# Strassen's seven products for q and z of five heads in a hybrid attention block

## The chip, the cores and the metric

The kernel runs on one core of a Trainium2 chip. The metric is the device time of one execution in microseconds (us). The core has five engines with a queue each: TensorE (PE, matrix products; PEld are its weight loads), VectorE (DVE), ScalarE (ACT), GpSimd (POOL) and SyncE (SP, which here only issues transfers). An engine takes its instructions in order; semaphores order the engines among each other.

## What is computed

One decoder block on 512 tokens of width 2048: RMSNorm, one wide input projection, two groups of attention heads side by side, a SiLU gate on each head's output, the output projection, a residual and a last RMSNorm.

```python
h = _rmsnorm(x, norm_g[l])
proj = h @ w_in[l]
(qa, kca, vca, ksa, vsa, kwa, vwa, za, ga, qb, kb, vb, zb) = jnp.split(proj, offsets, axis=-1)
...
y_a = o_a.reshape(B, S, WIDTH_A) * jax.nn.silu(za)
...
y_b = o_b.reshape(B, S, WIDTH_B) * jax.nn.silu(zb)
x = x + jnp.concatenate([y_a, y_b], axis=-1) @ w_out[l]
return _rmsnorm(x, final_g)
```

The A group has 8 heads of 128 in two groups of four that share keys and values; each head sums a compressed, a selected and a windowed attention with gates `ga`. The B group has 16 heads of 64 with a window and sinks. What matters here: each A head needs a 128-wide slice of q (rotated) and a 128-wide slice of z (the gate), both products of the same normalized x with two slices of `w_in`.

## The kernel before

Precision: every fp32 factor is split into a high part, rounded to fp32r by ACT, and a low part, the difference formed by DVE. A product is then three matmuls, high x high, high x low and low x high (`mm3`, lines 91 to 94). x is held transposed in `xh` and `xl`: 16 tiles (k) of 128 rows of the model width by 512 tokens, with the norm's gain already multiplied in.

A weight slice of 128 columns comes in two transfers of 512 KB (`load_unit`, lines 59 to 71: a transfer on SP into `raw`, the high part at L68 on ACT, the low part at L69 on DVE; three buffers of each). `proj` makes one slice of q or z from it: 16 tiles x 3 matmuls of 512 columns into one of two PSUM banks (`pj`). `q_evac` rotates q (three DVE multiplications, one POOL addition) and splits it; `z_evac` forms z(1 + tanh(z/2)).

The A heads run in a loop: z of head h, `attn_a(h)`, q of head h + 1. `attn_a` makes four score tiles (L408) in one PSUM tile of three banks, masks them and finds the row minimum on DVE (L410, L414), exponentiates on ACT (L420, L424), scales the rows on DVE (`pc` at L430, `tt` at L433), transposes them on TensorE (L443), splits them (L377, L378) and multiplies with the values (L450 to L452, L465, L467); `finish` multiplies with the gate into `yt[h]`, which stays in SBUF up to the output projection. Before the A heads, a first stage (in its own memory `p0`) makes keys, values and the compressed blocks; after them come the B heads and the output projection, which already makes three of its four column blocks by Strassen's seven products.

The text is written in one order, and a planner with a model of the times lays out each engine's order before the run: an instruction that is ready is taken ahead of an earlier one that is not. So TensorE fills the pauses of `attn_a` with the projections that follow it, and transfers go out when their buffer is free by that plan. A tile's buffer is given to the next tile of its tag when every access to the old one has ended. The number of buffers (`bufs`) thus sets how far work can run ahead.

Of the kernel before, what the change touches and what calls it, by code (L numbers as in the profile page):

```python
# [10 lines left out]
F32 = mybir.dt.float32  # L11
F32R = mybir.dt.float32r
# [16 lines left out]
WARM = 40  # L29
TAB_W = 512 + NQ * CMP + 256 + 1  # L30
# [3 lines left out]
def hybrid_block(ctx, tc, xT, xtm, w0, w1s, w2s, wz, wkb, wo0, wos, cw1, cw2, cpos, rope, tabs, sinks, gT, fg, out):  # L34
# [18 lines left out]
    vbf = const.tile([P, NQ, P], F32, name="vbf")  # L53
# [30 lines left out]
    VH = kv.tile([P, NQ, 2, 256], F32R, name="VH")  # L84
    VL = kv.tile([P, NQ, 2, 256], F32R, name="VL")
# [18 lines left out]
    gt = s0.tile([P, KT], F32, name="gt")  # L104
# [168 lines left out]
    def v_evac(t, w, ps):  # L273
        vt = VF[:, t // 2, w, :] if t % 2 else tmp("vt")[:, 0:256]
        act.activation(vt, ps[:, 0:256], AF.Copy, scale=rstd[:, t:t + 1])
        act.activation(VH[:, t, w, :], vt, AF.Copy)
        pool.tensor_tensor(out=VL[:, t, w, :], in0=vt, in1=VH[:, t, w, :].bitcast(F32), op=ALU.subtract)

# [21 lines left out]
    def proj(src):  # L300
        ps = psp.tile([P, S], F32, name="pj", tag="pj")
        for u in range(2):
            hi, lo = load_unit(src[:, u], 1024)
            for j in range(8):
                k = 8 * u + j
                mm3(ps, hi[:, j * P:(j + 1) * P], lo[:, j * P:(j + 1) * P], xh[:, k, :], xl[:, k, :], k == 0,
                    k == KT - 1)
        return ps

    q0 = proj(wz[0])  # L310
    for t in range(NQ):
        v_evac(t, 1, sacc2[t])
        act.activation(vbf[:, t, :], sacc2[t][:, 256:384], AF.Copy, scale=rstd[:, t:t + 1])
        dve.tensor_scalar(gates[:, t, :], sacc2[t][:, 384:408], rstd[:, t:t + 1], None, op0=ALU.mult)
    act.activation(gates, gates, AF.Tanh, scale=0.5)
# [19 lines left out]
    ypair = []  # L335
# [9 lines left out]
    def q_rope(ps, cos, sin):  # L345
        t1 = wk.tile([P, S], F32, name="t1", tag="t1")
        t2 = wk.tile([P, S], F32, name="t2", tag="t2", bufs=1)
        rope_mul(t1, t2, ps, cos, sin)
        pool.tensor_tensor(out=t1, in0=t1, in1=t2, op=ALU.add)  # L349
        return t1  # L350

    def q_evac(ps, cos, sin):
        t1 = q_rope(ps, cos, sin)
        qh = wk.tile([P, S], F32R, name="qh", tag="qh")
        ql = wk.tile([P, S], F32R, name="ql", tag="ql")
        act.activation(qh, t1, AF.Copy)
        pool.tensor_tensor(out=ql, in0=t1, in1=qh.bitcast(F32), op=ALU.subtract)
        return qh, ql

    def finish(h, op, st):  # L360
        if h % 2 == 0:
            ypair.append(yp.tile([P, 2, S], F32, name=f"yp{h // 2}", tag=f"yp{h // 2}"))
        yt[h] = ypair[h // 2][:, h % 2, :]
        dve.scalar_tensor_tensor(out=yt[h], in0=op, scalar=0.5, in1=st, op0=ALU.mult, op1=ALU.mult)
# [20 lines left out]
    def attn_a(h, qh, ql, st):  # L385
# [4 lines left out]
        for pair in range(2):  # L390
# [5 lines left out]
            for i in range(2):  # L396
# [9 lines left out]
                for pi, (qq, kk) in enumerate(((qh, KH), (qh, KL), (ql, KH))):  # L406
                    for (a, b, ko) in groups:
                        pe.matmul(sp[:, a:b], qq[:, qs], kk[g][:, ko:ko + b - a], start=pi == 0, stop=pi == 2)  # L408
# [19 lines left out]
            for i in range(2):  # L428
                qt = 2 * pair + i
                dve.tensor_scalar(pc[:, qt], tc_[:, qt, :].unsqueeze(1).to_broadcast([P, 4, CMP]), dn[:, i, 0:1], None,  # L430
                                  op0=ALU.mult)
            for (i, w, tv) in views:
                dve.tensor_scalar(tv, tv, dn[:, i, 1 + w:2 + w], None, op0=ALU.mult)  # L433
# [4 lines left out]
            for bi in range(0, len(blocks), 2):  # L438
# [7 lines left out]
                for e in range(2):  # L446
                    w, kt = blocks[bi + e]
                    vs = slice(g * P, g * P + P)
                    es = slice(e * 256, e * 256 + 256)
                    pe.matmul(oc, VH[:, kt, w, vs], ph[:, es], start=first, stop=False)  # L450
                    pe.matmul(oc, VH[:, kt, w, vs], pl[:, es], start=False, stop=False)  # L451
                    pe.matmul(oc, VL[:, kt, w, vs], ph[:, es], start=False, stop=False)  # L452
                    first = False
# [15 lines left out]

    for h in range(8):  # L470
        if h == 0:
            qh, ql = q_evac(q0, cosA, sinA)
        st = z_evac(proj(wz[8 + h]))
        cur = (qh, ql)
        attn_a(h, *cur, st)
        if h < 7:
            qh, ql = q_evac(proj(wz[h + 1]), cosA, sinA)
# [13 lines left out]
    dve.tensor_tensor(out=sinB, in0=sinB, in1=rstdb, op=ALU.mult)  # L491
    sk = wb.tile([P, 2, 16], F32, name="sk")
# [25 lines left out]
    def qb_evac(ps):  # L518
        t1 = q_rope(ps, cosB, sinB)
        q2 = []  # L520
        for v in range(2):
            qs = wk.tile([P, S], F32R, name="qs", tag="ql" if v else "qh")
# [85 lines left out]
    for i in range(8):  # L608
# [13 lines left out]
        attn_b(i, tts, st)  # L622
    wbs.close()
# [18 lines left out]
    H0, H1 = slice(0, 256), slice(256, 512)  # L642
# [113 lines left out]
    for n in range(1, 4):  # L756
# [104 lines left out]
        else:  # L861
# [8 lines left out]
            def pair():  # L870
                return [wp.tile([P, 1024], F32R, name=nm, tag=nm) for nm in ("whi", "wlo")]
# [175 lines left out]
```

## Time and profile before

| | us |
|---|---|
| median of 3 runs | 845.5 |
| lowest, highest | 844.88, 845.76 |
| the profiled execution | 844.82 |
| its span, first to last instruction | 842.7 |

The granted TensorE clock was 0.997 over the span. The profile counts, for each engine, busy time and instructions, what ended its idle time, and for groups of instructions the number, the mean duration and the idle time before them. Durations of neighbouring instructions on one engine overlap, on TensorE above all, so the distance between two starts is the rate. L12 is line 12 of the kernel; a line can be that of a helper. Stages by time: the first stage to 194, the A heads from there to 478, the B heads to about 700, the output projection to the end.

### The profile page before, as it was taken

The numbers are of one execution on the slowest core, as the hardware profiler recorded it, in microseconds if no ns is written. First come the engines' busy times: TensorE is split into PE (matmuls) and PEld (weight loads), VectorE is DVE, ScalarE is ACT, GpSimd is POOL, SyncE is SP. The second block draws the span as 40 slices with busy tenths as digits, with TensorE's granted clock in tenths as the row PEclk, the third lists the DMA queues.
The fourth block names the chain that finished last, engine by engine and source line by source line (L and its number), as shares of the span: only waits on it lengthen the run. The fifth ranks groups of instructions, "written<-read, shape, count | busy, mean of one in ns | idle before, by whom it ended". The sixth has DMA issues, their size and how long they took to land.

```text
span 842.7 us, 12725 instructions
## 1 busy us (share of the span) xinstructions
PE 832.5 (99%) x4774; PEld 727.4 (86%) x4774; DVE 600.4 (71%) x1240; ACT 408.9 (49%) x853; POOL 93.3 (11%) x69
## 2 busy tenths in 40 slices
PE   9999999999999999999999999999999999999996
PEld 7788899988888888888888888888888788999996
DVE  7869364745676766665776688877677798777895
ACT  6634245443555444444343456444444647543545
POOL 4500002011110110110111210111011000000000
PEclk9999999999999999999999999999999999999998
DMA  9642275532221122121221222222222227896935
GB/s 325 205 130 78 83 223 181 170 126 75 75 74 52 52 74 70 56 56 71 88 88 52 75 77 74 76 75 75 75 76 79 72 75 254 222 254 171 265 62 200
DMA packets 32909, 98.25 MB, mean 117 GB/s; under 512 B 3920, under 2 KB 3920, under 8 KB 32848
## 3 DMA queue, kind: packets, MB, share of 16 engines
q1 hardware_dynamic: 30832, 90.63, 32.8%
q0 software_dynamic: 1728, 6.29, 4.3%
q8 instruction: 37, 0.61, 0.3%
q10 hardware_dynamic: 288, 0.52, 0.2%
q14 instruction: 24, 0.20, 0.1%
HBM read 93.24 MB, written 4.19 MB: 116 GB/s over the span
## 4 chain that ended last, share of the span: by engine, by line
PE 93%; DMA 3%; ACT 1%; DVE 1%; issue 1%; POOL 0%; SPq 0%; DVEq 0%; ACTq 0%
PE pj L93 17%; PE pj L92 17%; PE pj L94 17%; PE oa L92 5%; PE oa L93 5%; PE oa L94 5%; PE bank L94 4%; PE sp L408 4%; PE bank L92 3%; PE bank L93 3%; DMA xr<-xT 2%; PE tp L443 2%; PE tp L583 1%; PE op L452 1%; PE op L451 1%; PE op L450 1%
## 5 line engine op out<-in xcount | busy, mean ns | idle before, releaser
L92 PE MATMUL pj<-xh,whi 128*128 128x512 f32 x560 | 222.5, 397 | 0.0
L94 PE MATMUL pj<-xh,wlo 128*128 128x512 f32 x560 | 221.9, 396 | 0.0
L93 PE MATMUL pj<-xl,whi 128*128 128x512 f32 x560 | 221.9, 396 | 0.0
L69 DVE TENSOR_TENSOR wlo<-raw,whi 128x1024 fp32r<-128x1024 f32 (+2 forms) x130 | 151.8, 1173 | 74.4 <-ACT whi L68 73.3
L68 ACT ACTIVATE whi<-raw 128x1024 fp32r<-128x1024 f32 (+2 forms) x129 | 124.8, 971 | 152.5 <-PE pj L93 68.9
L93 PEld LDWEIGHTS pj<-xl,whi 128*128 128x128 f32 x560 | 105.5, 188 | 22.4 <-issue 0.9
L94 PEld LDWEIGHTS pj<-xh,wlo 128*128 128x128 f32 x560 | 105.5, 188 | 22.3
L92 PEld LDWEIGHTS pj<-xh,whi 128*128 128x128 f32 x560 | 105.4, 188 | 21.8 <-issue 0.2
L349 POOL TENSOR_TENSOR t<-t,t 128x512 f32<-128x512 f32 x17 | 36.6, 2151 | 395.8 <-DVE t L99 377.2
L378 DVE TENSOR_TENSOR pl<-tp,ph 128x512 fp32r<-128x512 f32 x56 | 37.9, 686 | 32.2 <-ACT ph L377 32.2
L377 ACT ACTIVATE ph<-tp 128x512 fp32r<-128x512 f32 x56 | 32.2, 594 | 52.5 <-PE tp L443 44.6
L92 PE MATMUL oa<-whi,yh 128*128 128x256 f32 (+1 forms) x168 | 50.9, 304 | 0.6 <-ACT yh L635 0.6
L93 PE MATMUL oa<-wlo,yh 128*128 128x256 f32 (+1 forms) x168 | 51.0, 303 | 0.0
L94 PE MATMUL oa<-whi,yl 128*128 128x256 f32 (+1 forms) x168 | 50.4, 303 | 0.0
L562 ACT ACTIVATE ttb<-ttb,mnb 128x256 f32<-128x256 f32 (+1 forms) x64 | 30.1, 472 | 22.9 <-DVE mnb L555 21.9
L93 PE MATMUL bank<-wlo,xh 128*128 128x256 f32 (+1 forms) x128 | 40.1, 315 | 0.0
L94 PE MATMUL bank<-whi,xl 128*128 128x256 f32 (+1 forms) x128 | 39.8, 313 | 0.0
L93 PE MATMUL bank<-xl,whi 128*128 128x512 f32 x96 | 37.4, 394 | 0.0
L92 PE MATMUL bank<-xh,whi 128*128 128x512 f32 x96 | 37.2, 398 | 0.1
L92 PE MATMUL bank<-whi,xh 128*128 128x256 f32 (+1 forms) x128 | 36.7, 315 | 0.4 <-ACT whi L68 0.4
L424 ACT ACTIVATE tt<-tt,mn 128x128 f32<-128x128 f32 (+3 forms) x64 | 35.3, 553 | 3.0 <-DVE mn L414 2.7
L92 PEld LDWEIGHTS oa<-whi,yh 128*128 128x128 f32 x168 | 31.6, 188 | 2.1 <-ACT yh L635 0.8
(297 smaller groups left out, 1771.4 us busy)
## 6 DMA issues: line engine op xcount, KB each, us to landing
raw<-wz SPq DMA_DIRECT2D x64, 512.0 KB, 3.7
raw<-cw SPq DMA_DIRECT2D x16, 512.0 KB, 3.7
raw<-wos SPq DMA_DIRECT2D x12, 512.0 KB, 4.3
rw<-wos SPq DMA_DIRECT2D x10, 512.0 KB, 5.9
xr<-xT SPq DMA_DIRECT2D x16, 256.0 KB, 5.4
raw<-w SPq DMA_DIRECT2D x8, 512.0 KB, 3.7
raw<-wo SPq DMA_DIRECT2D x8, 512.0 KB, 3.6
raw<-w SPq DMA_DIRECT2D x15, 256.0 KB, 4.8
```

What stands on the lines that cost most here:

```text
L68: act.activation(hi[:, :width], raw[:, :width], AF.Copy)
L69: last["lo"] = dve.tensor_tensor(out=lo[:, :width], in0=raw[:, :width], in1=hi[:, :width].bitcast(F32), op=ALU.subtract).ins
L92: pe.matmul(ps, ah, bh, start=first, stop=False, skip_group_check=go_on)
L93: pe.matmul(ps, ah, bl, start=False, stop=False, skip_group_check=go_on)
L94: recent["mm"] = pe.matmul(ps, al, bh, start=False, stop=last, skip_group_check=go_on).ins
L349: pool.tensor_tensor(out=t1, in0=t1, in1=t2, op=ALU.add)
L377: act.activation(ph, tp, AF.Copy)
L378: dve.tensor_tensor(out=pl, in0=tp, in1=ph.bitcast(F32), op=ALU.subtract)
L408: pe.matmul(sp[:, a:b], qq[:, qs], kk[g][:, ko:ko + b - a], start=pi == 0, stop=pi == 2)
L424: act.activation(tv, tv, AF.Exp, bias=mn[:, i, 1 + w:2 + w], scale=-1.0, accum_out=dn[:, i, 1 + w:2 + w])
L443: pe.transpose(tp[:, e * 256 + i * P:e * 256 + i * P + P], views[2 * i + w][2][:, kt * P:(kt + 1) * P], ident)
L562: act.activation(tv, tv, AF.Exp, bias=mn[:, e, v:v + 1], scale=-1.0, accum_out=dn[:, e, v:v + 1])
```

## The change

Heads 0 to 2 keep their projections; heads 3 to 7 (`FIRST = 3`) get q and z from `pair`. Strassen's scheme takes the two weight slices as two columns of a 2 x 2 block matrix, whose rows are the odd and the even k tiles, and the two halves of 256 tokens (`H0`, `H1`) of x likewise. Seven products of 8 tiles x 3 matmuls of 256 columns replace eight block products. Three of the seven x factors are parts of x as they are ("12", "21", "22"); four are sums of parts ("p", "u", "q", "w").

- `build(m)`, eight times in heads 0 to 2, loads two x tiles again, combines them with the gain and splits the sums. "p" and "u" go to the SBUF memory of `yt`; "q" to the memory of the second group's keys and values; "w" is written to DRAM (`wd`). All builds use one buffer, `raw4`.
- What was there goes to DRAM meanwhile: the second group's keys and values (`Kd`, `Vd`), `vbf`, the first half of the even x tiles (`xd`), and the outputs of heads 0 to 7 (`yd`), written by `finish`.
- `swap_x(wd)` overwrites the first half of the even x tiles with "w" before head 3, `swap_x(xd)` brings x back after head 7. The second group's keys and values are loaded over the first group's after head 3, so `attn_a` always reads index 0. `y_back` loads the outputs in B heads 1 to 4.
- `pair` loads three quarters of the weights and adds others to them by accumulating transfers from POOL (`more`), makes seven units, and sums the products in two PSUM banks and two SBUF tiles.
- The row scalings of `attn_a` move from DVE to ACT, in all heads for `tt`, from head 3 on for `pc`. The loop's order is now q, z (or `pair`), then attention. `proj` takes the odd tiles of each half first.
- `t1`, `ql` and its user in the B heads have one buffer instead of two.

```diff
-            for j in range(8):
+            for n, j in enumerate((1, 3, 5, 7, 0, 2, 4, 6)):
...
+    even = [x.rearrange("p (m e) s -> p e m s", e=2)[:, 0, :, 0:256].bitcast(F32) for x in (xh, xl)]
+    for e in range(2):
+        nc.sync.dma_start(Kd[e], (KH, KL)[e][1].bitcast(F32))
+        nc.sync.dma_start(Vd[e], (VH, VL)[e][:, 1].rearrange("p t w c -> p (t w c)").bitcast(F32))
+    nc.sync.dma_start(vbd, vbs)
...
             for (i, w, tv) in views:
-                dve.tensor_scalar(tv, tv, dn[:, i, 1 + w:2 + w], None, op0=ALU.mult)
+                act.activation(tv, tv, AF.Copy, scale=dn[:, i, 1 + w:2 + w])
...
+    def split(hi, lo, src):
+        act.activation(hi, src, AF.Copy)
+        last["lo"] = dve.tensor_tensor(out=lo, in0=src, in1=hi.bitcast(F32), op=ALU.subtract).ins
+
+    def build(m):
+        xr = wk.tile([P, 2, S], F32, name="raw4", tag="raw4", bufs=1)
+        nc.sync.dma_start(xr, xT[:, 2 * m:2 * m + 2, :])
+        ge, go = [gt[:, 2 * m + e:2 * m + e + 1] for e in range(2)]
+        a11, a21, a12, a22 = xr[:, 0, H0], xr[:, 0, H1], xr[:, 1, H0], xr[:, 1, H1]
+        act.activation(xr[:, 1, :], xr[:, 1, :], AF.Copy, scale=go)
+        dve.tensor_tensor(out=a21, in0=a11, in1=a21, op=ALU.subtract)
+        dve.scalar_tensor_tensor(out=a11, in0=a11, scalar=ge, in1=a12, op0=ALU.mult, op1=ALU.subtract)
+        dve.scalar_tensor_tensor(out=a12, in0=a21, scalar=ge, in1=a12, op0=ALU.mult, op1=ALU.subtract)
+        dve.tensor_tensor(out=a22, in0=a22, in1=a12, op=ALU.add)
+        split(*xf["p", m], a11)
+        for nm, src, scale in (("u", a12, -1.0), ("q", a21, ge)):
+            hi, lo = xf[nm, m]
+            act.activation(hi, src, AF.Copy, scale=scale)
+            dve.scalar_tensor_tensor(out=lo, in0=src, scalar=scale, in1=hi.bitcast(F32), op0=ALU.mult, op1=ALU.subtract)
+        split(a11.bitcast(F32R), a22.bitcast(F32R), a22)
+        nc.sync.dma_start(wd[0, :, m], a11)
+        nc.sync.dma_start(wd[1, :, m], a22)
...
+    def ring():
+        turn[0] += 1
+        if turn[0] % 4 == 0:
+            return wk.tile([P, 1024], F32, name="raw4", tag="raw4", bufs=1)
+        return wp.tile([P, 1024], F32, name="raw", tag="raw")
...
+    def prod(bank, u, op, new):
+        for m in range(8):
+            cs = slice(m * P, m * P + P)
+            ah, al = xf[op, m]
+            mm3(bank, u[0][:, cs], u[1][:, cs], ah, al, new and m == 0, m == 7, not new)
...
+        x1 = load(3)
+        u0 = unit(x1)
+        x2 = load(0)
+        u3 = unit(x2)
+        more(x2, 2)
+        more(x1, 2)
+        prod(pb[:, H0], u0, "22", True)
+        act.activation(d, pb[:, H0], AF.Copy, scale=-1.0)
+        x3 = load(1)
+        prod(pa[:, H0], u3, "p", True)
+        plus(d, d, pa[:, H0])
+        u2 = unit(x3)
+        prod(pb[:, H0], u2, "21", False)
+        act.activation(zr[:, H1], pb[:, H0], AF.Copy)
+        plus(jj, d, zr[:, H1])
+        u4 = unit(x2)
+        more(x2, 3)
+        prod(pa[:, H0], u4, "12", False)
+        act.activation(qv[:, H0], pa[:, H0], AF.Copy)
+        plus(jj, jj, qv[:, H0], ALU.subtract)
+        u1 = unit(x1)
+        prod(pa[:, H1], u1, "w", True)
+        plus(d, d, pa[:, H1])
+        u5 = unit(x2)
+        plus(x2, x2, x3)
+        prod(pb[:, H1], u5, "u", True)
+        plus(d, d, pb[:, H1])
...
+        qq = q_split(qv)
+        u6 = unit(x2)
+        prod(pb[:, H1], u6, "q", False)
+        plus(jj, jj, pb[:, H1])
+        plus(zr, zr, rstdb, ALU.mult)
...
+    for e in range(2):
+        nc.sync.dma_start(xd[e], even[e])
     for h in range(8):
-        if h == 0:
-            qh, ql = q_evac(q0, cosA, sinA)
-        st = z_evac(proj(wz[8 + h]))
...
+        if h < FIRST:
+            qq = q_evac(q0 if h == 0 else proj(wz[h]), cosA, sinA)
+            st = z_evac(proj(wz[8 + h]))
+        else:
+            if h == FIRST:
+                swap_x(wd)
+            qq, st = pair(h)
+        if h < FIRST:
+            build(3 * h)
+        attn_a(h, *qq, st)
+        if h < FIRST:
+            for m in range(3 * h + 1, min(3 * h + 3, 8)):
+                build(m)
+        if h == 3:
+            for e in range(2):
+                nc.sync.dma_start((KH, KL)[e][0].bitcast(F32), Kd[e])
...
+    swap_x(xd)
```

128 lines of the change are left out of this document (97 added, 31 removed).

## The prediction

> **What bounds the kernel now.** I read the page's shares first, then the chain of waits, then busy time by stretches.
>
> ```profile
> span 842.7 us, 12725 instructions
> PE 832.5 (99%) x4774; PEld 727.4 (86%) x4774; DVE 600.4 (71%) x1240; ACT 408.9 (49%) x853; POOL 93.3 (11%) x69
> ...
> PE 93%; DMA 3%; ACT 1%; DVE 1%; issue 1%; POOL 0%; SPq 0%; DVEq 0%; ACTq 0%
> ```
>
> TensorE is busy for 99% of the span and makes 93% of the chain that ended last. A change pays if it takes matmul columns away and leaves TensorE fed. The stretches show how much room the other engines have (columns: stretch, its length, then PE, PEld, DVE, ACT, POOL busy, clock, DMA share, GB/s):
>
> ```profile
> 730.00:760.00 30.00, 30.00 (x255) 30.00 (x254) 20.69 (x23) 14.12 (x19) 3.49 (x4) 1.00 0.89 244
> 700.00:730.00 30.00, 30.00 (x192) 27.02 (x190) 26.32 (x49) 21.55 (x48) 1.93 (x2) 1.00 0.84 273
> 667.00:700.00 33.00, 32.44 (x150) 26.35 (x150) 31.08 (x63) 19.09 (x34) 0.00 (x0) 1.00 0.27 80
> 210.00:437.00 227.00, 227.00 (x1241) 194.78 (x1240) 151.37 (x422) 104.59 (x272) 24.51 (x14) 1.00 0.21 68
> ```
>
> The last row is the stage of the A heads: TensorE never pauses, DVE is busy 67%, ACT 46%. From 700 to 730 TensorE is still full beside DVE at 88% and ACT at 72%; from 667 to 700, with DVE at 94%, it loses 0.56 us.
>
> **What the change removes.** A head's q and z are 2 x 48 matmuls of 512 columns; the seven products are 7 x 24 of 256 columns. Starts, not durations, give the rate, since matmuls overlap:
>
> ```profile
> 312.86 0.39 PE L92 MATMUL pj<-xh,whi 128*128 128x512 f32 x1
> ...
> 321.22 0.39 PE L92 MATMUL pj<-xh,whi 128*128 128x512 f32 x1
> ```
>
> 36 matmuls lie between these starts: 8.36/36 = 0.232 us each. The row 730 to 760 above is the output projection's own seven products, all of 256 columns and each with a new weight: 30/255 = 0.118 us. A head falls from 96 x 0.232 = 22.3 to 168 x 0.118 = 19.8 us, 2.5 less; five heads (3 to 7) give **-12.3 us** if nothing else moves.
>
> The row shows PEld busy for all of those 30 us, and still one matmul per 0.118 us. The Trainium skill (TensorE: Matmul & The Clock Gate, The mechanism) says that a weight load overlaps a running matmul only in another row group or in the background weight buffer; the first reading would make the small matmuls dear and is the last rival below, the second leaves the sum as it is, and the row is on its side.
>
> **Work beside it, heads 3 to 7.** A head's period and the attention's share of it:
>
> ```profile
> 291.03 0.40 PE sp L408 x3
> ...
> 421.49 0.40 PE sp L408 x3
> ```
>
> These are the first scores of heads 3 and 7: 130.46/4 = 32.6 us per head, of which 22.3 is q and z, so attention is 10.3 on TensorE. The new period is 30.1. The prices of the small work:
>
> ```profile
> L69 DVE TENSOR_TENSOR wlo<-raw,whi 128x1024 fp32r<-128x1024 f32 x98 | 121.6, 1242 | 60.3 <-ACT whi L68 59.5
> L68 ACT ACTIVATE whi<-raw 128x1024 fp32r<-128x1024 f32 x98 | 103.8, 1059 | 137.4 <-PE pj L93 62.9 <-issue 36.5 <-PE bank L94 22.9
> L650 DVE TENSOR_TENSOR yp<-yp 128x256 f32<-128x256 f32 x8 | 3.4, 421 | 0.1
> L462 ACT ACTIVATE pcr<-tp 128x256 fp32r<-128x256 f32 x16 | 6.0, 377 | 0.0
> L424 ACT ACTIVATE tt<-tt,mn 128x512 f32<-128x512 f32 x16 | 11.4, 714 | 1.0 <-DVE mn L414 1.0
> L424 ACT ACTIVATE tt<-tt,mn 128x128 f32<-128x128 f32 x16 | 6.2, 388 | 0.0
> ```
>
> ```profile
> 215.40 0.48 DVE L430 TENSOR_SCALAR pc<-tc__1868,dn 128x128 f32<-128x128 f32 x2
> 215.79 1.00 DVE L433 TENSOR_SCALAR tt<-tt,dn 128x128 f32<-128x128 f32 x4
> ...
> 228.31 1.54 DVE L433 TENSOR_SCALAR tt<-tt,dn 128x384 f32<-128x384 f32 x4
> ```
>
> DVE per head is 0.67 x 32.6 = 21.7 now. Seven units instead of four add 3 x 1.24 lows; the sum of x2 and x3 adds 1.2, six half-width sums 6 x 0.42. The scalings leave for ACT: 1.00 + 1.54 and 2 x 0.48. That makes 21.7 + 3.7 + 1.2 + 2.5 - 3.5 = 25.6 of 30.1 us, 85%. ACT: 15.0 + 3 x 1.06 + 3 copies of 0.38 + 8 scalings at the mean of the two L424 rows, 0.55, + 4 of 0.39 = 25.3, 84%. DVE lies below the 88% at which TensorE stayed full; ACT lies above its 72%. I cost throughput at nothing because of that stretch; if the cover fails, it is the second rival.
>
> What the pair cannot hide by itself is its **handovers**. The products share two PSUM banks: 12 and then w go to pa, u and then q to pb's other half, and the next head's 22 waits for q's last sum. At each, TensorE waits for an evacuation (0.42 on DVE or 0.38 on ACT) that itself waits for its engine; I take 0.9 us, one such operation and about half a split ahead of it. Three per head, 15 in all: 0 if attention matmuls always stand ready (10.3 of 30.1 us are such), 13.5 if never. I take a quarter, +3.4: attention holds a third of the period, and its matmuls come in short bursts that are often ready somewhere near.
>
> The step from 12 to w counts only if a bank cannot be read and written at once. The Trainium skill (PSUM — Partial Sum Buffer, Summary: rules for kernel authors) says to read another bank while a matmul runs; by it three handovers count, without it two and the term would be 1.1 less. No row of before shows one bank used in both ways at once.
>
> **The combinations, heads 0 to 2.** Each of eight builds loads 512 KB of x into the one buffer raw4, combines it there and writes two parts to DRAM from it. So the next load waits for the writes: a chain of eight links.
>
> ```profile
> 192.83 1.18 DVE L331 TENSOR_TENSOR VC<-vc,VC 32x128 fp32r<-32x128 f32 x4 [0.40 <-ACT VC L329]
> 194.14 0.69 DVE L97 TENSOR_TENSOR t<-pj,cosA 128x512 f32<-128x512 f32 x1
> ...
> 197.87 0.69 DVE L340 TENSOR_TENSOR zr<-pj,rstdb 128x512 f32<-128x512 f32 x1 [1.64 <-POOL t L349]
> ```
>
> ```profile
> 709.00 0.42 DVE L640 TENSOR_TENSOR ul<-yp,uh 128x256 fp32r<-128x256 f32 x1
> ...
> 710.34 0.42 DVE L640 TENSOR_TENSOR ql<-yp,qh 128x256 fp32r<-128x256 f32 x1
> ```
>
> ```profile
> raw<-wz SPq DMA_DIRECT2D x64, 512.0 KB, 3.7
> late<-xtm SPq DMA_DIRECT2D x6, 512.0 KB, 10.4
> out<-xs SPq DMA_DIRECT2D x4, 256.0 KB, 2.3
> ...
> GB/s 325 205 130 78 83 223 181 170 126 75 75 74 52 52 74 70 56 56 71 88 88 52 75 77 74 76 75 75 75 76 79 72 75 254 222 254 171 265 62 200
> ```
>
> The buffer lies where the first stage's tiles are; the q rotation, the first user of that memory, started at 194 only, right behind that stage's last operation. One link: load 3.7; one 512-wide ACT scaling 0.7 (the L424 row); seven dependent half-width DVE operations, one per 0.335 us by the two rows 1.34 apart (four steps), 2.4; a write 2.3. That is 9.1 undisturbed. The waits behind other work are unknown: 0 at best, and 3.3 if each of three entries (ACT, DVE, ACT) finds a split of 1.06 to 1.24 ahead of it. I take a third, 1.1, as most instructions there are shorter: 10.2 a link, 194 + 82 = 276 for the last write.
>
> Then half of the even tiles is overwritten with the combined part, 2.1 MB. At 265 GB/s, the highest late slice, 8 us; as four transfers of 3.7 one behind the other, 15; late<-xtm at 10.4 per 512 KB gives 42, in a stretch that moves 244 to 273 GB/s. I take 9, near the first, as this stage moves 68 GB/s: ready at 285. TensorE comes to product w at 197.9 (z of head 0 done, the L340 row) + four projections 44.6 + three attentions 30.9 + four products 11.3 = 284.7. So it is **just in time**; I put +1.
>
> DVE in those heads: 21.7 - 2.5 + 8 x 8 x 0.335/3 = 26.3 of 32.6, 81%; ACT 15.0 + 4.4 + 8 x (0.7 + 4 x 0.38)/3 = 25.3, 78%; covered as above.
>
> **The DRAM traffic.** xd, the second group's K and V and vbf are some 4.5 MB of writes that depend on finished tiles and can go in the slack of earlier slices (75 GB/s), at no cost. The group's reload waits for head 3's last score (K) and last value matmul (V), 1.1 MB each, 4 to 8 us, under pair 4. x comes back after head 7's w, under two products (5.7), attention 7 (10.3) and the odd tiles, which the new projection order takes first. On SP all these can stand ahead of weight loads; raw tiles are loaded up to three ahead. Bounds 0 and the 15 us of one bare swap; I take +1 for all. The y transfers, eight of 256 KB each way, lie beside heads with slack.
>
> The pair's accumulating loads:
>
> ```profile
> ch<-wos POOLq DMA_DIRECT2D x6, 512.0 KB, 8.9
> rw<-wos POOLq DMA_DIRECT2D x6, 512.0 KB, 5.7
> ```
>
> x2 goes through load 3.7, four splits 4 x 2.3, two accumulations of 5.7 to 8.9, a sum 1.2 and the last product 2.8: 28 to 35 us. Its buffer is free once the head before has split u1, about 21 + half an attention = 5 + 11 us before that head's end; with the period that is 46. At least 11 us of slack: +0.
>
> **Sum**: 844.82 (span 842.7 and 2.1 around it) - 12.3 + 3.4 + 1 + 1 = 837.9. The median of the runs is 0.7 above this execution: **838.5**.
>
> **Rivals.**
> 1. *The builds are late* (slower). All entries wait 3.3: a link of 12.4, the last write at 293, w ready at 302 and 17.5 us late: 844.8 - 12.3 + 17.5 + 4.4 = 854.4. It decides from the link at which the delay eats the 7.9 us left of the gain: (284.7 + 7.9 - 194 - 9)/8 = 11.2 us. For it: one buffer, and two engines at 80%. Against: dependent half-width operations run 0.335 apart at 709 to 710 beside a full TensorE.
> 2. *The pair's own work is the bound* in every head: ACT at 84% with every split behind attention. If x2's ten engine steps wait 1.5 us each beyond the 11 us of slack, a head grows by about 4: 844.8 - 12.3 + 20 + 1 = 853.5. For it: ACT's 84% has no precedent in this trace. Against: DVE's 94%.
> 3. *Gain and losses cancel*: a link near 11.2, 845.
> 4. *Weight loads do not hide*:
>
> ```profile
> L93 PEld LDWEIGHTS pj<-xl,whi 128*128 128x128 f32 x560 | 105.5, 188 | 22.4 <-issue 0.9
> ```
>
> 168 x (0.188 + 0.118) is 51 per head, five heads 145 slower, 990. The 730 to 760 row is against it.
>
> **How the numbers follow.** Forecast 0.50 (833 to 843), rival 1 0.28, rival 2 0.12, rival 3 0.09, rival 4 0.01. Low end: all losses hidden, 844.8 - 12.3 = 832.5, so 833. High end 855 takes in rival 1's and 2's centres. A difference below 0.2% (1.7 us) cannot be told from none. Faster 0.52 (the forecast and the lower edge of rival 3), same 0.09 (the rest of rival 3 and the lower edge of rival 1), slower 0.39 (rivals 1, 2 and 4).
>
> **What would show it.** Starts 0.118 apart in the products; seven of them and attention at 30 to 31 us a head; raw4 loads 10.2 apart, the last write before 280, and TensorE without a gap ahead of the first w. A gap of over 8 us between 262 and 310 proves rival 1; periods of 33 and more between heads 3 and 7, ACT above 90%, prove rival 2. The prediction is wrong if TensorE idles more than 12 us in the A heads.

## The result and the profile after

| | before | after |
|---|---|---|
| median, us | 845.19 (844.57 to 845.76) | **886.11** (885.22 to 890.62, 4 runs) |
| the profiled execution | 844.82 | 890.62 |
| its span | 842.7 | 888.9 |
| matmuls | 4774 | 5134 |
| granted TensorE clock, mean | 0.997 | 0.978 |

The ratio is 1.0489 (1.0453 to 1.0524): 41 us slower, where 838.5 was predicted and 855 was the upper end. From here on lines are those of the kernel after, which lie some 30 further down from line 350 on: scores L438, row scalings L462 to L466, the rounding `ph` L407, a pair's weight splits L514 and L515, its accumulating loads L564, the first operations of a build L522 to L525, its two writes L533 and L534.

The page of after (shares, the clock row, the chain of waits):

```profile
span 888.9 us, 13847 instructions
PE 841.0 (95%) x5134; PEld 749.4 (84%) x5134; DVE 632.8 (71%) x1270; ACT 477.1 (54%) x1007; POOL 100.6 (11%) x84
...
PEclk9999999999989799899999999999999999999998
...
PE 70%; DMA 14%; DVE 8%; ACT 4%; issue 3%; POOL 0%; SPq 0%; ACTq 0%; POOLq 0%; DVEq 0%
```

TensorE's part of the chain fell from 93% to 70%, and transfers rose from 3% to 14%. The clock row dips from its twelfth slice on. Stretches of the same trace (stretch, its length, busy time of PE, PEld, DVE, ACT and POOL, clock, DMA share, GB/s):

```profile
210.00:437.00 227.00, 196.51 (x1342) 180.17 (x1342) 155.55 (x381) 140.59 (x345) 30.96 (x27) 0.94 0.50 125
256.00:260.00 4.00, 0.00 (x0) 0.00 (x0) 0.43 (x1) 0.70 (x2) 0.00 (x0) 0.92 0.50 165
260.00:264.00 4.00, 3.05 (x14) 3.03 (x14) 3.89 (x14) 3.94 (x13) 0.00 (x0) 0.50 0.00 0
264.00:268.00 4.00, 4.00 (x24) 3.87 (x24) 3.97 (x8) 2.25 (x7) 0.00 (x0) 0.72 0.11 37
332.00:336.00 4.00, 4.00 (x36) 4.00 (x35) 0.80 (x1) 0.46 (x3) 0.00 (x0) 1.00 0.96 173
```

The first row is the stretch in which TensorE never paused before; now it stands for 30.5 us of 227. The next three are one pause and its price: TensorE runs nothing from 256 to 260, then matmuls run at half clock, and full speed is back only in the stretch that ends at 268. The last row is a pair undisturbed. The row counts matmuls that only reach into it too, so the rate is read from starts:

```profile
332.00 0.28 PE L103 MATMUL pj<-xh,whi 128*128 128x256 f32 x1
...
333.06 0.28 PE L103 MATMUL pj<-xh,whi 128*128 128x256 f32 x1
```

Nine matmuls lie between these starts: 0.118 us each, as predicted.

The loss by kind, profile against profile, is 46.2 us of span. Busy time should have been 832.5 - 12.3 = 820.2 and is 841.0, 20.8 more. The granted clock was one half in six pieces between 259 and 519, 34 us in all, in which TensorE was busy for 30; at full clock that work would have taken half the time, so an estimated 15 of the 20.8 are lowered clock. The other 6 are not explained by a run; a matmul that runs alone is counted with its whole length (0.28 us), one in a stream adds 0.118. Pauses of over 0.3 us between 190 and 560 add up to 35.0, where before had none. Less the 12.3 that makes 43.5; shorter pauses are most of the rest.

Where it begins, by the issues of SyncE's queue for the builds (start, duration of the issue):

```profile
194.19 0.33 SPq L519 DMA_DIRECT2D raw<-xT  x1
...
210.02 0.33 SPq L519 DMA_DIRECT2D raw<-xT  x1
...
223.65 0.33 SPq L519 DMA_DIRECT2D raw<-xT  x1
...
235.57 0.33 SPq L519 DMA_DIRECT2D raw<-xT  x1
...
253.51 0.33 SPq L519 DMA_DIRECT2D raw<-xT  x1
...
269.08 0.33 SPq L519 DMA_DIRECT2D raw<-xT  x1
...
285.55 0.33 SPq L519 DMA_DIRECT2D raw<-xT  x1
...
297.87 0.33 SPq L519 DMA_DIRECT2D raw<-xT  x1
...
305.64 0.32 SPq L534 DMA_DIRECT2D wd<-raw  x1
306.78 0.59 SPq L617 DMA_DIRECT2D xh<-wd  x1
```

Seven links take 103.7 us: 14.8 each, not 10.2. The last write goes out at 305.6, not 276, the swap behind it. Product w is not the only one that waits. "p", the second product of a pair, also needs one tile of each build:

```profile
L103 PE MATMUL pj<-pu,whi x8: 278/283/382, 269.0 to 303.9; 128*128 128x256 f32 x8
```

This is the group view of the `pu` tiles up to 306 (duration in ns least, median and most, then first and last start). Eight k tiles that need 2.8 us of TensorE lie over 35 us: five run between 269.0 and 272, the other three at 278.17, 293.35 and 303.90, each within 1 us of ScalarE's rounding of its tile (the eighth at 302.92). Until then neither "12" (it adds to p's bank) nor, in the planned order, what follows it starts, so TensorE has little to put into the pauses of attention. And attention itself stops, in the timeline of after:

```profile
259.30 0.43 DVE L523 TENSOR_TENSOR raw<-raw 128x256 f32<-128x256 f32 x1 [8.42 <-DMA raw<-xT]
259.30 0.72 ACT L522 ACTIVATE raw<-raw,gt 128x512 f32<-128x512 f32 x1 [8.05 <-DMA raw<-xT]
...
260.32 0.57 ACT L407 ACTIVATE ph<-tp 128x512 fp32r<-128x512 f32 x1
...
260.95 0.58 PE L482 MATMUL op<-ph,VH 128*128 128x256 f32 x1 [5.93 <-ACT ph L407]
```

ScalarE and VectorE take their instructions in the planned order. Both stood eight microseconds at the first instruction of a build whose load, issued at 253.51, took 5.8 us. The rounding of attention's transposed scores was behind it on ScalarE, and TensorE waited for that. The waits of after between 190 and 515 (us in all, times, longest):

```profile
DVE wlo L515 <- ACT whi L514: 29.1, 15, 5.9
...
ACT whi L514 <- DMA raw<-wq: 27.4, 7, 6.9
DVE raw L523 <- DMA raw<-xT: 21.6, 7, 8.4
ACT raw L522 <- DMA raw<-xT: 19.4, 6, 8.1
```

Two loads that hold two in-order engines: the builds' x (`xT`) and the pairs' weights (`wq`).

### The profile page after: what moved, and what is told of

Read it like the earlier page. It is cut to its first block, busy times and chain, and to the rows that moved or that the text cites. A ratio compares the mean times of both kernels' runs of the same rounds, so it can differ in the third digit from the quotient of the medians.

```text
span 888.9 us, 13847 instructions
## 1 busy us (share of the span) xinstructions
PE 841.0 (95%) x5134; PEld 749.4 (84%) x5134; DVE 632.8 (71%) x1270; ACT 477.1 (54%) x1007; POOL 100.6 (11%) x84
## 3 DMA queue, kind: packets, MB, share of 16 engines
q1 hardware_dynamic: 43552, 109.58, 37.7%
q0 software_dynamic: 3888, 14.16, 9.5%
## 4 chain that ended last, share of the span: by engine, by line
PE 70%; DMA 14%; DVE 8%; ACT 4%; issue 3%; POOL 0%; SPq 0%; ACTq 0%; POOLq 0%; DVEq 0%
PE pj L103 11%; PE pj L104 11%; PE pj L105 11%; DMA raw<-wq 5%; PE oa L103 4%; PE oa L105 4%; PE oa L104 4%; PE bank L103 4%; PE bank L104 4%; PE bank L105 4%; DMA raw<-xT 3%; DMA wd<-raw 3%; DVE wlo L515 2%; PE tp L748 1%; DMA xh<-xd 1%
## 5 line engine op out<-in xcount | busy, mean ns | idle before, releaser
L103 PE MATMUL pj<-xh,whi 128*128 128x512 f32 (+1 forms) x560 | 206.3, 368 | 8.3 <-DMA xh<-xd 3.2
L104 PE MATMUL pj<-xl,whi 128*128 128x512 f32 (+1 forms) x560 | 205.6, 367 | 2.5 <-DMA xl<-wd 2.5
L105 PE MATMUL pj<-xh,wlo 128*128 128x512 f32 (+1 forms) x560 | 204.8, 366 | 0.0
L80 DVE TENSOR_TENSOR wlo<-raw,whi 128x1024 fp32r<-128x1024 f32 (+2 forms) x110 | 125.6, 1149 | 72.7 <-ACT whi L79 71.9
L79 ACT ACTIVATE whi<-raw 128x1024 fp32r<-128x1024 f32 (+1 forms) x109 | 103.5, 953 | 116.0 <-PE pj L104 39.8
L104 PEld LDWEIGHTS pj<-xl,whi 128*128 128x128 f32 x560 | 107.1, 191 | 19.3 <-DMA xl<-wd 2.7
L105 PEld LDWEIGHTS pj<-xh,wlo 128*128 128x128 f32 x560 | 107.3, 192 | 15.7
L515 DVE TENSOR_TENSOR wlo<-raw,whi 128x1024 fp32r<-128x1024 f32 x35 | 46.2, 1324 | 31.9 <-ACT whi L514 29.1
L514 ACT ACTIVATE whi<-raw 128x1024 fp32r<-128x1024 f32 x35 | 36.8, 1053 | 39.6 <-DMA raw<-wq 27.4
L366 POOL TENSOR_TENSOR t<-t,t 128x512 f32<-128x512 f32 x12 | 24.4, 2037 | 207.3 <-DVE t L110 188.6
L407 ACT ACTIVATE ph<-tp 128x512 fp32r<-128x512 f32 x56 | 32.3, 589 | 19.2 <-PE tp L476 12.8
```

What stands on the lines that cost most here:

```text
L79: act.activation(hi[:, :width], raw[:, :width], AF.Copy)
L80: last["lo"] = dve.tensor_tensor(out=lo[:, :width], in0=raw[:, :width], in1=hi[:, :width].bitcast(F32), op=ALU.subtract).ins
L103: pe.matmul(ps, ah, bh, start=first, stop=False, skip_group_check=go_on)
L104: pe.matmul(ps, ah, bl, start=False, stop=False, skip_group_check=go_on)
L105: recent["mm"] = pe.matmul(ps, al, bh, start=False, stop=last, skip_group_check=go_on).ins
L407: act.activation(ph, tp, AF.Copy)
```

## The experiments

Where nothing else is said a kernel has one time, beside 844.6 to 845.7 of the kernel before on the same chip; differences of 2 us between such single times are not used.

**Which half of the change costs.** e1: no builds and no swap for w, so its products p, u, q and w read other data; e2: the builds alone.

```diff
# e1: "p", "u" read other parts of xh and xl
...
-            if h == FIRST:
-                swap_x(wd)
             qq, st = pair(h)
-        if h < FIRST:
-            build(3 * h)
         attn_a(h, *qq, st)
-        if h < FIRST:
-            for m in range(3 * h + 1, min(3 * h + 3, 8)):
-                build(m)
# e2: every head by proj, as before
...
-            if h == FIRST:
-                swap_x(wd)
-            qq, st = pair(h)
+        qq = q_evac(q0 if h == 0 else proj(wz[h]), cosA, sinA)
+        st = z_evac(proj(wz[8 + h]))
...
-    swap_x(xd)
```

> Left out: the eight builds, their DRAM parts and the first swap; the products p, u, q and w read parts of x or of K and V instead of the sums. Everything else is as in the changed kernel (five heads of seven products, accumulated weights, K, V, y and x through DRAM). Theory A (two separate losses: in the changed kernel TensorE's pauses and its lowered clock before 320 us cost about 26 us and belong to the builds, those after it about 28 us and belong to the pairs, against the 12 gained): 845 - 12 + 28 - 3 for the swap = 858, range 853 to 865. Rival B (the builds cause all, and the late start disturbs the pairs that follow): 833 to 840.

> Left out: the seven products; heads 3 to 7 make q and z as before, and both swaps of x are gone. The eight builds run in heads 0 to 2 and nobody uses them; K, V and y go through DRAM and the scalings are on ACT as in the changed kernel. Theory A: the builds' loss stays whatever follows, 845 + 26 = 871, or less where the waiting projections can run past the builds: 855 to 871. Rival C (the builds hurt only because head 3 must wait for the last of them and because the accumulated loads of the pairs cross them): 845 to 849, with no gap of over 2 us ahead of 300.

e1 took **843.38**, e2 **846.23** (before 845.73). e1 lies between its two expectations, e2 in its rival's. Neither half alone explains 41 us: the pairs alone are a little faster, the builds alone nearly free. In e2 the last write goes out at 304.4, as late as in after, and the engines stand for the loads of x almost as long:

```profile
DVE raw L523 <- DMA raw<-xT: 20.5, 8, 4.0
...
ACT raw L522 <- DMA raw<-xT: 16.4, 7, 4.8
```

Yet TensorE's pauses from 190 to 310 add up to 4.6 us there, for it had projections that need no build. So the length of the chain does not come from the pairs, and the chain costs only where TensorE depends on it. In e1, throughput holds too (stretch as above):

```profile
303.00:403.00 100.00, 98.01 (x800) 95.64 (x800) 77.45 (x189) 76.29 (x193) 17.44 (x15) 1.00 0.57 138
```

**What makes the chain long.** e3 leaves the accumulating loads out; e4 makes the builds from `xh` + `xl` in SBUF, with no load and no scaling; e6 puts all three builds of a head ahead of its attention; e5 has pairs in heads 4 to 7 only, with the builds where they were.

```diff
# e3
-            pool.dma_start(t, src[quarter], accum_op=ALU.add)
+            pass
# e4
...
-        nc.sync.dma_start(xr, xT[:, 2 * m:2 * m + 2, :])
-        act.activation(xr[:, 1, :], xr[:, 1, :], AF.Copy, scale=go)
+        dve.tensor_tensor(out=xr, in0=xh[:, ks, :].bitcast(F32), in1=xl[:, ks, :].bitcast(F32), op=ALU.add)
...
# e5
-FIRST = 3
+FIRST = 4
...
-        if h < FIRST:
+        if h < 3:
             build(3 * h)
         attn_a(h, *qq, st)
-        if h < FIRST:
+        if h < 3:
# e6
-            build(3 * h)
+            for m in range(3 * h, min(3 * h + 3, 8)):
+                build(m)
         attn_a(h, *qq, st)
-        if h < FIRST:
-            for m in range(3 * h + 1, min(3 * h + 3, 8)):
-                build(m)
```

> Left out: the fifteen accumulating loads, so products 12, w, u and q use weights without those terms. Rival C (those loads fill the transfer engines, delay the builds' loads and writes and the pairs' units): 850 to 862, writes of the builds back at 1.8 us each. Theory A: the builds are late anyway, only the pairs' waits for their weights go: 870 to 880.

> The builds add the high and low part of x in SBUF (one DVE addition of 1024 columns) in place of the 512 KB load and of the ACT scaling. So no engine waits for a load at a build's start and a link of the chain is 4 us shorter. Theory A (the builds' loss comes from ACT and DVE standing at the build's first instruction until its load lands, 20 us each in the profile): most of the 26 goes, 862 to 870. Rival D (DVE is short of time, one more addition a build makes it worse): 886 or more.

> One size changed: the pairs begin with head 4 instead of head 3; the eight builds stay in heads 0 to 2, so their last write (307 us in the changed kernel) comes 20 us ahead of the first product that needs them. Theory E (the whole loss is that head 3 runs out of work ahead of the builds; builds alone cost 0.5 us, pairs alone gain 2.3): 845.7 - 4 x 0.5 = 843 to 846. Rival F (builds and pairs disturb each other on the transfer engines and on ACT wherever they meet, and K and V come back while a pair runs): 855 to 875.

> One order changed: all three builds of a head stand ahead of its attention in the program, so the planner prefers them to the attention's instructions. Theory E with the builds' pace set by their place behind attention on DVE and ACT (7.2 us between load and last write, of which 3.1 are the build's own): a link falls from 14.2 to 10 or 11 us, the last write to 275 to 285, the time to 848 to 858. Rival G (the pace is the load, the write and the one buffer): last write still after 300, 880 to 890.

Measured: e3 874.89 (in theory A's range), e4 871.17 (1 us above it), e5 863.02 and e6 884.79 (in their rivals' ranges). Neither the contention nor the load is the chain's main part: without accumulating loads the swap still starts at 302.4, without the builds' own load at 300.8. Yet e3 and e4 give back 11.2 and 14.9 us with a swap only 4 and 6 us earlier, so a part of the loss is not the chain's length; that it is engines standing at a load fits the waits above, but the two edits change other work too. The order in the text changes nothing (306.9). What is common to all is one buffer between entry and write. e5 moves the need instead: the swap still starts at 305.6, but head 3 no longer waits for it, and 23 us come back. That pairs 4 to 7 still cost 18 us over before spoke for a second cause.

**The buffer.** e7 gives every second build a weight buffer.

```diff
-        xr = wk.tile([P, 2, S], F32, name="raw4", tag="raw4", bufs=1)
+        pool_of, kind = ((wk, dict(name="raw4", tag="raw4", bufs=1)), (wp, dict(name="raw", tag="raw")))[m % 2]
+        xr = pool_of.tile([P, 1024], F32, **kind).rearrange("p (e s) -> p e s", e=2)
```

> Every second build takes one of the three raw buffers of the weights instead of raw4, so the next load need not wait for the last build's writes. Rival G: a link falls by load and write, 6.9 us, for half of the builds and more; last write at 270 to 285, 850 to 865. Theory E (the place on DVE and ACT): last write at 295 or later, 870 to 890, and a little more wait for weights.

**861.68**, in rival G's range, with the last write (257.9) earlier than it gave. The swap, in SyncE's issues of e7, comes 46 us earlier, and 24.4 us come back:

```profile
175.44 0.33 SPq L520 DMA_DIRECT2D raw<-xT  x1
...
260.55 0.59 SPq L618 DMA_DIRECT2D xl<-wd  x1
261.24 0.80 SPq L618 DMA_DIRECT2D xh<-wd  x1
```

Two things make it earlier. A weight buffer does not lie in the first stage's memory, so one build loads at 175.44, 19 us ahead of the first load of after, and has its writes out by 195.3. The other seven take 63 us from the next load, 9.0 each. ScalarE and VectorE also stand at the builds' loads for 13.2 and 10.1 us instead of 19.4 and 21.6. That one buffer costs 24 us is shown, by taking it away; how much of it is the lateness and how much the standing is not divided. 17 us over the kernel before are left.

**What is left.** On top of e7: e8 gives the last key rotation (the projection of the B keys that runs at head 7's end) a tile of its own instead of the single `t1`; e9 leaves the accumulating loads out (e3's edit); e10 puts the `tt` scalings back on VectorE.

```diff
# e8
-    def q_rope(ps, cos, sin):
-        t1 = wk.tile([P, S], F32, name="t1", tag="t1", bufs=1)
+    def q_rope(ps, cos, sin, tag="t1"):
+        t1 = wk.tile([P, S], F32, name="t1", tag=tag, bufs=1)
...
-    act.activation(kb1, q_rope(proj(wkb), cosB, sinB), AF.Copy)
+    act.activation(kb1, q_rope(proj(wkb), cosB, sinB, "zr"), AF.Copy)
# e10
-                act.activation(tv, tv, AF.Copy, scale=dn[:, i, 1 + w:2 + w])
+                dve.tensor_scalar(tv, tv, dn[:, i, 1 + w:2 + w], None, op0=ALU.mult)
```

> Base is the kernel with two buffers for the builds (861.7). One edit: the first rotation of the B heads takes the buffer of zr, so the next rotation does not wait for the only t1 until attention 7 has ended. Theory H (the pause of 3 to 3.6 us at the end of the A heads, and the low clock behind it, come from the one t1): the pause goes, 857 to 859. Rival (the rotation stands behind attention 7's last instruction on DVE anyway): pause unchanged, 861 to 863.

> Base as in e8; left out: the fifteen accumulating loads, so products 12, w, u and q lack those terms. Theory I (what is left between this kernel and the pairs alone, 18 us, is ACT and DVE standing at a split until an accumulated weight lands): 846 to 852. Rival J (it is the handovers and attention's own steps on ACT and DVE, with no work for TensorE between them): 857 to 862.

> Base as in e8; one edit: the scalings of tt go back to DVE in all heads (2.5 us a head off ACT's 4.4). Rival J in the form that the moved scalings lengthen attention (two changes of engine more, behind ACT's splits): 850 to 857, no wait of TensorE for the scaling at its transposes. Theory I: 861 to 868, as DVE is the fuller engine in heads 0 to 2.

854.13, 850.83 and 853.60: -7.5, -10.9 and -8.1 against e7. e8 gains more than its theory gave, e9 and e10 lie in the ranges of theory I and of rival J. What the accumulating loads do is seen in the stretch of the pairs, of e7 and of e9:

```profile
303.00:403.00 100.00, 93.06 (x741) 90.24 (x739) 74.09 (x167) 66.34 (x166) 16.19 (x15) 0.98 0.50 119
```

```profile
303.00:403.00 100.00, 98.73 (x811) 96.75 (x811) 78.45 (x184) 75.03 (x183) 9.62 (x6) 1.00 0.28 91
```

Without them TensorE is busy for 98.7 of 100 us, and VectorE and ScalarE are busier, not less: it was waiting, not throughput. The pause that e8 takes away is the last one in TensorE's timeline of after (2.9 us; 3.6 in e7, none there in e8):

```profile
514.55 0.50 PE L103 MATMUL pj<-xh,whi 128*128 128x512 f32 x1 [2.90 <-DVE t L110]
```

**Do they add up, and what is the limit?** e11 is e7 + e8 + e10 (5 runs). e12 is e11 with one plain load and three GpSimd sums in place of the accumulating loads (4 runs). e13 is e1 with e8's edit.

```diff
# e12
-        def more(t, quarter):
-            pool.dma_start(t, src[quarter], accum_op=ALU.add)
+        def sums(out, a, b):
+            pool.tensor_tensor(out=out, in0=a, in1=b, op=ALU.add)
...
-        more(x2, 2)
-        more(x1, 2)
+        x4 = load(2)
+        sums(x1, x1, x4)
+        sums(x4, x4, x2)
...
-        u4 = unit(x2)
-        more(x2, 3)
+        u4 = unit(x4)
+        sums(x2, x2, x1)
```

> Two buffers for the builds, a tile of its own for the last key rotation, and the row scalings back on VectorE: the three edits of e7, e8 and e10 in one kernel. Alone, on top of two buffers (861.7), the second gave -7.5 and the third -8.1. If they save different pauses: 844 to 848. Rival (both fill the same waits, so only the larger counts): 851 to 855.

> As e11, and the three accumulating loads of a pair become one plain load and three sums on GpSimd (a 512-wide sum took it 2.04 us, so about 4.1 each, 12 of 30 us). Leaving the accumulating loads out altogether gave -10.9 (e9 against e7). If it is the transfer's 6.4 us and its share of the DMA engines that hold ACT: 836 to 842, faster than the kernel before. Rival (a sum of 4.1 us on GpSimd is as late as the transfer was): 844 to 850.

> e1 (no builds, x not swapped for w; the factors p, u, q and w read other data, so the output differs) with a tile of its own for the last key rotation. e1 had a pause of 3.3 us at its end from that shared tile. If pause and lowered clock go, as in e8: 837 to 840, the limit of the pairs with their accumulating loads. Rival (the pause moves to the rotations of the pairs): 842 to 844.

e11: **849.8**, ratio 1.0073 (1.0048 to 1.0098), -11.9 where the two edits alone gave 15.6: between theory and rival, they share part of a wait. e13: **839.29**, inside the theory's 837 to 840; -4.1 against e1.

e12: **869.1**, ratio 1.0291 (1.0273 to 1.0308), worse than both expectations. The group of VectorE's rotation products between 303 and 440, first in e11, then in e12 with GpSimd's sums below (count, busy, mean ns):

```profile
L603 DVE TENSOR_TENSOR t<-t,sinA 64x512 f32<-64x512 f32 x8 | 5.5, 686 | 0.2
```

```profile
L604 DVE TENSOR_TENSOR t<-t,sinA 64x512 f32<-64x512 f32 x8 | 13.2, 1653 | 0.2
...
L565 POOL TENSOR_TENSOR raw<-raw 128x1024 f32<-128x1024 f32 x10 | 25.3, 2526 | 75.1 <-DVE wlo L515 32.8 <-DVE dn L455 23.7 <-DVE mn L444 18.4
```

The same eight multiplications take 2.4 times as long on average: four are unchanged at 0.68 to 0.69 us, four take 2.1 to 2.8, each with a sum running beside it for 1.5 us or more. VectorE as a whole is busy for 671.1 us in e12 and 647.7 in e11. By the Trainium skill (SBUF — State Buffer, Who interferes with whom) a VectorE instruction with two inputs in SBUF contends with a GpSimd one that reads SBUF, and the rows agree. e12 also takes a fourth weight buffer for each pair; what of its 19.3 us over e11 is due to that was not tried.

**One transfer behind another.** e11's largest pause, 7.6 us at 272, hangs on a transfer that no theory had named. ScalarE's and VectorE's timeline of e11, then the DMA view of the same stretch (KB each, median us to landing):

```profile
277.35 0.63 ACT L358 ACTIVATE st<-zr 128x512 f32<-128x512 f32 x1 [9.23 <-DMA yd<-st]
...
278.02 0.69 DVE L359 SCALAR_TENSOR_TENSOR st<-st,zr 128x512 f32<-128x512 f32 x1 [9.30 <-ACT st L358]
```

```profile
xl<-wd SPq DMA_DIRECT2D x1, 1024.0 KB, 8.0
xh<-wd SPq DMA_DIRECT2D x1, 1024.0 KB, 12.7
...
yd<-st SPq DMA_DIRECT2D x1, 256.0 KB, 12.6
```

The write of head 0's output was issued 0.7 us behind the swap, on the same queue, and its tile is needed for head 2's gate. e14 is e11 with these writes on ScalarE's queue (10 runs):

```diff
-            nc.sync.dma_start(yd[h], st)
+            nc.scalar.dma_start(yd[h], st)
```

> e11 with the writes of the heads' outputs (yd) on ScalarE's DMA queue instead of SyncE's. In e11 the largest pause left (7.6 us at 272) follows ScalarE's wait of 9.2 us for the write of head 0's output, which took 12.6 us because it was issued 0.7 us behind the 2 MB that overwrite the even x tiles, on the same queue; VectorE stood behind it. If the queue is the cause, the pause falls to 2 us or less, with the lowered clock: 838 to 843, faster than before. Rival (the write shares the DMA engines with the 2 MB and is as late, or TensorE then waits for the 2 MB itself): 847 to 851.

```profile
yd<-st ACTq DMA_DIRECT2D x1, 256.0 KB, 5.5
```

The write, issued between the swap's two transfers (264.48), lands in 5.5 us instead of 12.6 and the pause is gone; no pause over 1.3 us is left in the A heads. The Trainium skill (DMA: Bandwidth & Descriptors, Queues, rings and completion order) says that a DMA engine goes round the queues packet by packet, and the two rows agree. But the time is **847.0**, ratio 1.0024 (1.0011 to 1.0037): not the 838 to 843 of the theory, and still 0.24% slower than before. In e14 TensorE still loses 8.4 us of the 113 between 190 and 303, beside a VectorE that is busy 83% there (69% before). e15 thins the builds: four heads by pairs, two builds in each of heads 0 to 3 (12 runs).

```diff
-FIRST = 3
+FIRST = 4
...
-            build(3 * h)
+            build(2 * h)
...
-            for m in range(3 * h + 1, min(3 * h + 3, 8)):
+            for m in (2 * h + 1,):
```

> e14 with four heads by pairs instead of five (4 to 7) and two builds in each of heads 0 to 3 instead of three, three and two in heads 0 to 2. It gives up 2.5 us of saved columns. In e14 TensorE lost 8.4 us of 113 from 190 to 303, in waits of about 1 us for VectorE, which was busy 83% there against 69% before; with two builds a head that falls to about 75%. If those waits come from the builds' density: 841 to 844. Rival (they come from the builds whatever their spacing, or from the weight buffers that the builds take): 846 to 850.

**844.4**, just above its theory's range, ratio 0.9999 (0.9984 to 1.0013): no difference from the kernel before. Stretches of e15:

```profile
190.00:303.00 113.00, 109.61 (x601) 92.95 (x600) 92.29 (x260) 66.18 (x172) 17.83 (x11) 1.00 0.49 145
...
338.00:403.00 65.00, 62.32 (x507) 60.40 (x506) 53.77 (x128) 38.96 (x98) 10.53 (x10) 1.00 0.56 128
```

TensorE's loss in the first stretch fell from 8.4 to 3.4, with VectorE still at 82%, so its load alone was not what mattered. But e15's first pair begins at 294.75 and e14's at 257.88, so the stretch differs by more than the builds' spacing; which waits went is not settled. No complete version of the scheme beat the kernel before.

## Why the prediction was wrong

Three kernels between before and after divide the 46.2 us between the profiled spans. A step can hold several edits, and each span is one execution (after's lies 4.5 above its median):

| step | span, us | difference |
|---|---|---|
| before | 842.7 | |
| pairs alone, own tile for the key rotation (e13) | 837.4 | -5.3 |
| the shared tile `t1` (e1) | 841.3 | +3.9 |
| builds and swap in time, two buffers (e7) | 859.9 | +18.6 |
| builds from one buffer (after) | 888.9 | +29.0 |

- **The gain, -12.3: right.** Starts are 0.118 apart; and in e13, where all seven products run, PE is busy 817.3 us, with 820.2 expected. There the first scores of heads 3 to 6 (294.06, 324.95, 356.13, 386.80) are 30.7 to 31.2 apart, with 30 to 31 expected. The weight loads hide; rival 4 is out.
- **Handovers, +3.4: right in size.** In e13's pairs, five matmuls start late by one (two behind `t` on ScalarE, two behind `t` on VectorE, one behind `tt`), 3.3 us together. Five of fifteen at 0.66 each come out as a quarter at 0.9 would; the quarter was a guess that held. The longest two:

```profile
298.38 0.39 PE L103 MATMUL pj<-xh,whi 128*128 128x256 f32 x1 [1.52 <-ACT t L579]
...
315.59 0.36 PE L103 MATMUL pj<-xh,whi 128*128 128x256 f32 x1 [0.73 <-ACT tt L454]
```

- **Throughput at nothing: right on the pairs' own work and on the builds alone** (e1: ScalarE 76%, VectorE 77%, TensorE 98%; e2: +0.5). Rival 2 as put, an engine at its limit, did not come: from head 3's first score to head 7's the periods of after are 36.2 us on average, over its 33, but ScalarE is busy for 63% there, not 90%.
- **The builds' link, 10.2: the step that failed.** It was 14.8. From a load's issue to the build's first operation it took 4.1 us on average (3.7 was put), from there to the first write's issue 6.0 (4.2: 3.1 of work and 1.1 of waits), and from there to the next load 4.3 (2.3). So the waits for ScalarE and VectorE, and the way out of the buffer, were mis-sized most. Even the upper bound of 12.4 was too low: it let three entries wait for one split each, but a build has five operations on ScalarE and eight on VectorE, all in the planned order of two busy engines, and two writes, the second 1.1 us behind the first. Rival 1 was right in kind and its condition (a link over 11.2) was met.
- **When the builds are needed, "just in time" at 284.7, failed as well.** The sum let TensorE run three whole attentions and four products ahead of w, and wait there once. But p, the second of the seven products and the first to need the builds, also needs every one of them; by the same sum, three products earlier, it comes at 276.2. And the planner takes the pair ahead of attention: in e13, with no builds to wait for, the first product starts at 255.35, ahead of head 2's first scores (257.24), and p at 259.98; in e14, with builds, p starts at 264.94. By these starts a last write at 276, as forecast, would have been late too.
- **The price of lateness was mis-sized.** The last write, issued at 305.64, lands at about 307.5 (the median of those writes is 1.9), which makes a link of 14.2 from 194. By rival 1's own sum that gives 194 + 113.6 + 9 = 316.6, 31.9 late, so 868.8. Measured was 886.1. p's wait and the in-order engines, which stopped attention too, are not in that sum. The predicted sign of rival 1, one gap of over 8 us between 262 and 310, never appeared; the 35 us are many pauses, 5.93 and 4.06 the longest. The sign of being wrong, over 12 us of idle TensorE, did: 30.5 between 210 and 437.
- **The clock was not in the sum at all.** About 15 us of busy time (the estimate above) came from half clock behind pauses. The Trainium skill (TensorE: Matmul & The Clock Gate, Part 1: The HAM clock gate) says that an idle window of about 3.4 us halves the clock until an equally long busy one has passed. The rows from 256 to 268 agree, and the prediction, which used that page for weight loads, did not apply this rule to its own late cases. But the clock of after also halved behind pauses of 1.9, 2.9 and 3.2 us, shorter than that window, and there the measurement decides:

```profile
398.50 0.33 PE L476 MATMUL tp<-ident,tt 128*128 128x128 f32 x1 [1.90 <-ACT tt L466]
```

```profile
399.40:402.70 3.30, 3.30 (x14) 2.95 (x14) 2.43 (x8) 3.30 (x8) 0.00 (x0) 0.50 0.00 0
```

- **Accumulating loads, +0: wrong by about 11 us** (e9 against e7, and e3 against after, 11.2). The slack was worked out for one weight buffer's life; what was late was ScalarE, which took the next split in order and stood for it: 27.4 us at the pairs' weights in after, 6.4 in e3.
- **One `t1`, and scalings on ScalarE: not priced as waits.** 4 to 7.5 us (e13 against e1, e8 against e7) and 8.1 (e10), the last two partly the same wait (e11).
- **DRAM traffic, +1: too little.** Bringing x back cost a pause of 3.2 us, and the write of a head's output behind the swap one of 7.6 in e11; e14, without it, was 2.8 us faster.

```profile
463.50 0.50 PE L103 MATMUL pj<-xh,whi 128*128 128x512 f32 x1 [3.21 <-DMA xh<-xd]
```

What stays open: the 7.7 us between e14 (847.0) and e13 (839.3). Their profiled executions differ by 9.9 us of span. 3.2 of it is idle time; between 190 and 560 TensorE's pauses add up to 12.5 us in e14 and 7.4 in e13, and the largest group in e14, 5.2 us, are transposes that wait for VectorE's scaling of `tt`. The other 6.7 are busy time (824.0 and 817.3), although e14's clock was never lowered before its last microseconds; no run explains it. e15, which gives up 2.5 us of saved columns and is still 2.6 faster than e14, suggests that it lies in how the builds are spread.

## What to carry to other kernels

A chain of load, compute and write through one buffer takes what the busiest in-order engines leave it, not the sum of its durations: count every operation of it as an entry into a queue, and look for the first consumer of its last link, which may be earlier than the one that the code names. Where engines run in a planned order, an instruction that waits for a transfer stops all work behind it; price the transfer's lateness by that work, and by the lowered clock that follows a pause of TensorE. Average shares of busy time (VectorE 71%, ScalarE 54% here) tell nothing of either.

## What the runs showed of the hardware

- TensorE's clock halved behind a pause of 5.9 us (0.50 from 260 to 264) and was back by 268. It halved also behind pauses of 4.1 us (0.50 from 293.5 to 303.7, with shorter pauses in between), 3.2 (464.3 to 467.6), 2.9 (515.5 to 518.8) and 1.9 us (399.4 to 402.7).
- An accumulating transfer holds the DMA engines longer than a plain one. Between 245 and 258 in after, by queue (packets, MB, share of 16 engines):

```profile
q0 software_dynamic: 288, 1.05, 58.9%
q1 hardware_dynamic: 411, 0.73, 15.1%
```

That is 56% per MB for the two accumulating loads and 21% for the rest, with smaller packets in the latter. Over the whole execution the ratio is smaller, about two: a share of 9.5% for the 14.16 MB of q0 and of 37.7% for the 109.58 MB of q1. From 252 to 256 the engines were 99% busy at 145 GB/s, in a kernel whose slices from the 34th to the 38th, in the output projection, move 176 to 277 GB/s.
- GpSimd's sums of 1024 columns took 2.5 us, less than the 4.1 worked out from its 512-wide row; VectorE was busy 23.4 us longer in that kernel (e12 against e11).
